# Spreading weight sums over an up-projection, forming one of them in the down stage, and accumulating a row convolution in PSUM by halves

## Chip, cores and metric

The kernel runs on one core of one Trainium2 chip. The metric is the device time of one execution in microseconds (us). Engines are named as in the profile: PE is TensorE, PEld its weight loads, DVE VectorE, ACT ScalarE, POOL GpSimd, SP the engine from whose queue every DMA of this kernel is issued. Each engine works through its instructions in program order.

## What is computed

Two layers of a streaming encoder for 1024 prompt rows and 128 sample rows (8 requests of 16), model width 1024, f32. Each layer has an attention part and the channel mixer on which this change works:

```
def conv_ffn(h, prev, w_up, conv_w, conv_b, w_down):
    u = h @ w_up
    ...
    ue = jnp.concatenate([prev.astype(u.dtype), u], axis=1)
    y = conv_b
    for tap in range(CONV_W):
        y = y + conv_w[tap] * ue[:, tap:tap + T]
    a, g = jnp.split(y, 2, axis=-1)
    out = (jax.nn.gelu(g) * a) @ w_down
    return out, ue[:, T:]
```

The up-projection gives 2 x 2816 columns; a causal convolution of width 3 runs along the rows; one half is gated by the GELU of the other; a down-projection goes back to 1024.

## The kernel before

Every f32 product is made of three matmuls: each operand is split into a high part (a cast, line 177, mostly on ACT) and the rest (a subtraction, line 188, mostly on DVE). Up- and down-projection use a scheme of seven block products in place of eight, which needs sums and differences of weight blocks and of activation blocks.

**The up stage** (`ffn`, layer 0 from about 490 to 1064 us, layer 1 from about 2020 to 2565 us). The 2816 columns are 22 blocks of 128, each a row `a` and a row `g`. The first two blocks are done the plain way (`plain`); the other twenty, j = 2 to 21, are pairs (`spair`). A pair loads two weight tiles through a ring of four tiles, forms the four weight sums S on POOL (lines 1177 to 1180), splits seven operands into a ring of six slots, and PE runs seven products of 24 matmuls (line 1229) into three groups of two PSUM banks, banks 0 to 5. A product's banks are read out (evicted) by ACT (lines 1188 and 1197) or by DVE (line 1190), and within a group the next product accumulates onto the banks only after that. Between the plain blocks and the first pair, `tsums` forms the matching sums of the activations on POOL and DVE.

`conv_row` then does the convolution for one row of 1152: one ACT activation with the third tap and the bias (line 1316), two DVE taps over the 1024 prompt columns (line 1277, called from `conv_row`), and the short taps of the samples with a small POOL addition (line 1286). The `g` row goes through GELU on ACT (line 1323) and a POOL multiplication (line 1324), and the result is stored to DRAM (`actD`). `act_sums` makes the four sums of two finished blocks on POOL (lines 1336 to 1339). In layer 0 `self.ada` runs in the background, four steps to a pair, with loads through the same ring of four tiles and PSUM bank 7.

`weight_sums(m)` makes the sums of the down weights, eleven times in a layer: two loads into the one pair of tiles `w0`, four POOL subtractions of 128 x 512 (lines 1348 to 1351), two stores of 512 KB to DRAM (`wT`). It is called in pairs 2, 3, 4, 6, 8, ..., 20, but it depends on nothing in a pair, and the order of the instructions is set by the tile framework's scheduler from its own timeline, not by the place of the call.

**The down stage** (`down`, 1065 to about 1340 us and 2566 us to the end). Seven products 1, 2, 5, 6, 3, 7, 4 run one after the other, each over eleven m; `fetch(q, m)` loads and splits activation and weight. For product 5 the weight is the difference held in the lower half of `wT[m, 0]`, loaded straight into the slot's low part. In layer 1 the last products run beside the final layer norm of eight row tiles (`head`, `tail`, `norm_last`); `homes` says in which buffer the residual row tile is loaded, and tiles 6 and 7 use the buffers that tiles 2 and 3 used before.

Of the kernel before, what the change touches and what calls it, by code (L numbers as in the profile page):

```python
# [12 lines left out]
AF = mybir.ActivationFunctionType  # L13
ALU = mybir.AluOpType
# [88 lines left out]
class Trunk:  # L103
# [1140 lines left out]
    def ffn(self, l, xsrc, xdst, affs):  # L1244
        nc, I, O, H, F = self.nc, self.I, self.O, self.H, self.F
        nc.sync.dma_start(self.cw, I["cw"][l])
        cw = self.cw.rearrange("p (c w) -> p c w", w=4)
# [22 lines left out]
        wide = Ring(self.ws.items + [F[:, 11644:12668], F[:, 8700:9724]])  # L1270
        narrow = self.ws
        ub = Ring([0, 1, 2, 3, 6, 7])
        UB = ((0, 384), (380, 388), (764, 388))

        def tapper(cc):
            def tap(o, u, i):
                nc.vector.scalar_tensor_tensor(o, u, cw[:, cc, i : i + 1], o, op0=ALU.mult, op1=ALU.add)  # L1277

            return tap

        def samples(y, u, cc, tap):
            y3 = y.rearrange("p (s q) -> p s q", q=16)
            u3 = u.rearrange("p (s q) -> p s q", q=16)
            tap(y3[:, :, 1:16], u3[:, :, 0:15], 1)
            tap(y3[:, :, 2:16], u3[:, :, 0:14], 0)
            nc.gpsimd.tensor_add(y3[:, :, 0:2], y3[:, :, 0:2], E4[:, cc])

        def rows(j, gg, src):
            uo = self.uo[gg].rearrange("p (j s r) -> p j s r", s=9, r=2)
            nc.scalar.copy(uo[:, j % 11], src.rearrange("p (s q) -> p s q", q=16)[:, :, 0:2])  # L1290
            if j % 11 == 10:
                nc.sync.dma_start(O["conv"][l, gg, j // 11], self.uo[gg])
# [20 lines left out]
        def conv_row(u, j, gg, y):  # L1313
            cc = j + 22 * gg
            tap = tapper(cc)
            nc.scalar.activation(y, u[:, 2:1154], AF.Identity, bias=cw[:, cc, 3:4], scale=cw[:, cc, 2:3])  # L1316
            tap(y[:, 0:1024], u[:, 1:1025], 1)
            tap(y[:, 0:1024], u[:, 0:1024], 0)
            samples(y[:, 1024:1152], u[:, 1026:1154], cc, tap)
            rows(j, gg, u[:, 1024:1168])  # L1320

# [22 lines left out]
        def weight_sums(m):  # L1344
            b11, b12, b21, b22 = (t[:, o : o + 512] for t in self.w0 for o in (0, 512))
            for i in range(2):
                nc.sync.dma_start(self.w0[i], I["wdn"][l, 2 * m + i])
            nc.gpsimd.tensor_sub(b11, b12, b11)
            nc.gpsimd.tensor_sub(b12, b22, b12)
            nc.gpsimd.tensor_sub(b22, b22, b11)  # L1350
            nc.gpsimd.tensor_sub(b21, b22, b21)
            for i in range(2):
                nc.sync.dma_start(self.wT[l][m, i], self.w0[i])

        def plain(j):
            y = [yact, ygate[j % 2]]
            for gg in range(2):
                w = self.wload(I["wup"][l, j + 22 * gg])
                for bi, (s0, n) in enumerate(UB):
                    ps = self.bank(ub.next())  # L1360
# [6 lines left out]
        def spair(j):  # L1367
            sa, sg = self.ws.next(), self.ws.next()
            nc.sync.dma_start(sa, I["wup"][l, j])
            nc.sync.dma_start(sg, I["wup"][l, j + 22])  # L1370
            ua, ug = us.next(), us.next()
            y = []

            def after(i, q):
                if i % 2 == 0:
                    self.step(1)
                if i == 1:
                    act_sums()
                if i == 2 and j in wsum:
                    weight_sums(wsum.index(j))  # L1380
                if q == 4:
                    y.append(ygate[j % 2])
                    conv_row(ug, j, 1, y[0])

            self.products(sa, sg, ua, ug, (S1, S2, S3), p1s, sub, TT, after, "first" if j == NPL else None)
            ya = yact
            conv_row(ua, j, 0, ya)
            gated(j, ya, y[0])

        self.pend = []  # L1390
        wsum = [2, 3] + list(range(4, NFF - 1, 2))
# [20 lines left out]
    def down(self, l, xsrc, xdst, affs, act_sums):  # L1412
        nc, I, F, H = self.nc, self.I, self.F, self.H
# [13 lines left out]
        narrow = self.ws  # L1427
        fa, fb = F[:, 4096:5120], F[:, 8320:9344]
        homes = {8: fa, 0: fb, 1: self.w0[1], 2: fa, 3: fb, 4: X2[:, 0:1024], 5: X2[:, 2048:3072], 6: fa, 7: fb}
        xs = {}  # L1430

        def rows(*ts):
# [3 lines left out]
        raws = [w[:, i * 512 : i * 512 + 512] for w in [self.w0[1]] + narrow.items for i in range(2)]  # L1436
        early = Ring(raws + [F[:, o : o + 512] for o in (0, 512, 1024)])
        late = Ring(raws)
        subs = self.subslots(ws[1:4])
        X1 = self.X1  # L1440
        acts = Ring([(X1[:, o : o + 640], X1[:, o + 640 : o + 1280]) for o in range(0, 8960, 1280)])
# [2 lines left out]
        wdn, wT, actD, actS = I["wdn"][l], self.wT[l], self.actD, self.actS  # L1444
        lo_half, hi_half = slice(0, 512), slice(512, 1024)

        def weight(src, ring=None):
            hi, lo = subs.next()
            raw = ring.next() if ring else lo.bitcast(F32)
            nc.sync.dma_start(raw, src)  # L1450
            self.split(raw, hi, lo, "a", "v")
            return hi, lo

        def act(src, sample=None):
            n = 512 if sample is None else 640
            hi, lo = (t[:, 0:n] for t in acts.next())
            raw = lo.bitcast(F32)
            nc.sync.dma_start(raw[:, 0:512], src)
            if sample is not None:
                nc.sync.dma_start(raw[:, 512:640], sample)  # L1460
            self.split(raw, hi, lo, "a", "v")
            return hi, lo
# [12 lines left out]
        def prompt(j, n):  # L1475
            return actD[j][:, n]

        def sample(j):
            return actD[j][:, 1024:1152]

        def fetch(q, m):
            e, o = 2 * m, 2 * m + 1
            w2 = None
            if q == 1:
                a, w = act(prompt(e, lo_half), sample(e)), weight(wdn[e][:, lo_half], early)
            elif q == 2:
                a, w = act(prompt(o, lo_half), sample(o)), weight(wdn[o][:, lo_half], early)
            elif q == 5:
                a, w = act(actS[m, 1][:, hi_half], sample(e)), weight(wT[m, 0][:, lo_half])
                w2 = weight(wdn[e][:, hi_half], late)  # L1490
            elif q == 6:
                a, w = act(actS[m, 0][:, lo_half], sample(o)), weight(wT[m, 1][:, hi_half])
                w2 = weight(wdn[o][:, hi_half], late)
            elif q == 3:
                a, w = act(actS[m, 1][:, lo_half]), weight(wdn[o][:, hi_half], late)
            elif q == 7:
                a, w = act(actS[m, 0][:, hi_half]), weight(wT[m, 0][:, hi_half])
            else:
                a, w = act(prompt(o, hi_half)), weight(wT[m, 1][:, lo_half])
            return a, w, w2 or w  # L1500
# [71 lines left out]
        aff = affs()  # L1572
# [23 lines left out]
        subs = Ring(subs.items + more)  # L1596
# [15 lines left out]
        subs = Ring(subs.items[0 : NK - len(more)] + more if l == 0 else subs.items)  # L1612
# [307 lines left out]
```

## Time and profile before

| | us |
|---|---|
| median of 3 runs | 2839.86 (2837.35 to 2843.75) |
| the profiled execution's own time | 2844.65 |
| its span (first to last instruction) | 2842.6 |
| PE busy in the span | 2676.1 (94%) |
| DVE busy | 2027.0 (71%) |
| ACT busy | 1348.0 (47%) |
| POOL busy | 1106.9 (39%) |
| mean granted PE clock | 0.975 |

All durations below come from the one profiled execution. The parts of its page and the answers of its trace that are used are: busy time by engine in a stretch, groups of instructions by line and shape (count, busy time, mean duration of one, idle time of the engine ahead of them and what ended it), the waits of one engine, and rows in order of time, where a bracket gives the idle time ahead of a row and what released it. F, X2 and H are large SBUF tensors cut up by hand, ws a weight tile, wh and wl the high and low part of a weight, xa an activation part, PS the PSUM banks, C small constants.

### The profile page before, as it was taken

The page shows a single profiled execution, that of the slowest core. Times are in us where ns is not written, and L with a number is a line of the kernel's source. Part 1 is how long each engine was busy: PE and PEld are TensorE (multiplying, and loading weights), DVE is VectorE, ACT ScalarE, POOL GpSimd, SP SyncE. Part 2 cuts the span into 40 slices and gives each one's busy share as a digit, 9 for nine tenths or more (in the row PEclk, how much of TensorE's full clock was granted, in tenths as well). Part 3 has the DMA queues.
Part 4 walks back from the last instruction along what each step waited for, and adds up shares of the span by engine and source line. Part 5 has one row for each costly group of instructions (what it writes and reads, how often), then busy time and mean ns, then how long its engine had stood idle before and what let it go on. Part 6 is the DMA issues. An engine that isn't in the chain of part 4 may idle for free. (4 is left out here: it accounts for less than half of the span.)

```text
span 2842.6 us, 47206 instructions
## 1 busy us (share of the span) xinstructions
PE 2676.1 (94%) x17134; PEld 2356.5 (83%) x17134; DVE 2027.0 (71%) x3850; ACT 1348.0 (47%) x2752; POOL 1106.9 (39%) x808
## 2 busy tenths in 40 slices
PE   7999889889999999999899999999988999999997
PEld 5897768878999997777798888767988999997775
DVE  4376767777776684588663677668888888885578
ACT  3475724433333344455636666652443344444454
POOL 2132523678554641013421111232489855551001
PEclk9999999999999999999999999999999999999998
DMA  8656434698554447675767457854565422237664
GB/s 291 213 159 197 141 129 156 209 329 283 183 175 156 163 133 236 225 248 196 267 201 257 122 156 198 225 162 146 178 206 196 177 81 96 85 116 239 216 218 156
DMA packets 252714, 534.35 MB, mean 188 GB/s; under 512 B 40032, under 2 KB 100400, under 8 KB 252480
## 3 DMA queue, kind: packets, MB, share of 16 engines
q1 hardware_dynamic: 252480, 531.32, 56.8%
q8 instruction: 135, 2.21, 0.3%
q14 instruction: 99, 0.81, 0.1%
HBM read 391.12 MB, written 149.54 MB: 190 GB/s over the span
## 5 line engine op out<-in xcount | busy, mean ns | idle before, releaser
L1229 PE MATMUL PS<-H,wh 128*128 128x256 f32 (+1 forms) x2624 | 409.7, 299 | 0.0
L1466 PE MATMUL PS<-wh,xa 128*128 128x512 f32 x1144 | 366.9, 399 | 11.9 <-DVE F L1584 5.3
L1229 PEld LDWEIGHTS PS<-H,wh 128*128 128x128 f32 x2624 | 374.4, 193 | 0.0
L1277 DVE SCALAR_TENSOR_TENSOR F<-F 128x1024 f32<-128x1024 f32 x320 | 312.9, 1025 | 28.1 <-ACT F L1316 27.8
L177 ACT CAST wh<-F 128x512 fp32r<-128x512 f32 (+2 forms) x234 | 137.1, 594 | 316.5 <-PE PS L1229 203.7
L1190 DVE TENSOR_TENSOR F<-PS,F 128x320 f32<-128x320 f32 (+1 forms) x446 | 196.6, 451 | 123.5 <-PE PS L1229 121.6
L188 DVE TENSOR_TENSOR wl<-F,wh 128x512 fp32r<-128x512 f32 (+2 forms) x234 | 238.6, 1029 | 56.0 <-ACT wh L177 54.3
L1466 PEld LDWEIGHTS PS<-wh,xa 128*128 128x128 f32 x1144 | 215.4, 189 | 69.5 <-ACT H L177 6.1
L1229 PE MATMUL PS<-H,wl 128*128 128x256 f32 (+1 forms) x1312 | 235.4, 301 | 24.4 <-ACT F L1197 15.3
L1466 PE MATMUL PS<-wl,xa 128*128 128x512 f32 x572 | 227.0, 397 | 0.2
L1229 PEld LDWEIGHTS PS<-H,wl 128*128 128x128 f32 x1312 | 196.6, 193 | 34.3 <-ACT F L1197 16.3
L1229 PE MATMUL PS<-xa,wh 128*128 128x320 f32 (+1 forms) x1328 | 207.5, 299 | 0.0
L188 DVE TENSOR_TENSOR xa<-xa 128x640 fp32r<-128x640 f32 (+1 forms) x154 | 122.5, 801 | 112.8 <-ACT xa L177 112.3
L1229 PEld LDWEIGHTS PS<-xa,wh 128*128 128x128 f32 x1328 | 189.8, 192 | 0.0
L1065 POOL TENSOR_TENSOR F<-F 128x1024 f32<-128x1024 f32 x24 | 62.7, 2611 | 308.2 <-ACT xa L177 148.9
L177 ACT CAST xa<-xa 128x640 fp32r<-128x640 f32 (+1 forms) x154 | 104.0, 682 | 162.8 <-DMA xa<-actD 110.8
L188 DVE TENSOR_TENSOR wl<-ws,wh 128x512 fp32r<-128x512 f32 (+1 forms) x149 | 166.2, 1120 | 10.3 <-ACT wh L177 10.2
L1316 ACT ACTIVATE F<-F 128x1152 f32<-128x1152 f32 x80 | 108.0, 1351 | 114.7 <-DVE F L1190 65.7
L177 ACT CAST wh<-ws 128x512 fp32r<-128x512 f32 (+1 forms) x167 | 113.1, 685 | 102.9 <-PE PS L1229 47.1
L640 POOL TENSOR_TENSOR F<-F,x2r 64x512 f32<-64x512 f32 x62 | 79.4, 1280 | 167.9 <-DVE F L616 145.6
L1324 POOL TENSOR_TENSOR F<-F 128x1152 f32<-128x1152 f32 x44 | 123.7, 2810 | 52.1 <-DVE F L1277 40.8
L1229 PE MATMUL PS<-xa,wl 128*128 128x320 f32 (+1 forms) x664 | 122.9, 307 | 21.2 <-DVE F L1190 20.7
(346 smaller groups left out, 6287.3 us busy)
## 6 DMA issues: line engine op xcount, KB each, us to landing
ws<-in_adaw_dram SPq DMA_DIRECT2D x64, 512.0 KB
ws<-in_wup_dram SPq DMA_DIRECT2D x49, 512.0 KB
F<-in_adaw_dram SPq DMA_DIRECT2D x48, 512.0 KB
w0f<-in_wdn_dram SPq DMA_DIRECT2D x44, 512.0 KB
wT<-w0f SPq DMA_DIRECT2D x44, 512.0 KB
actS<-F SPq DMA_DIRECT2D x44, 512.0 KB
xa<-actS SPq DMA_DIRECT2D x88, 256.0 KB
F<-in_wup_dram SPq DMA_DIRECT2D x39, 512.0 KB
```

The source lines that it names most:

```text
L177: nc.scalar.copy(out, in_)
L188: self.eng(el).tensor_sub(lo, src, hi.bitcast(F32))
L640: self.eng("v" if last else "p").tensor_mul(on[r, q], on[r, q], rb[r, :])
L1065: self.eng(er[0]).tensor_mul(xr, x, self.lng)
L1190: nc.vector.tensor_add(d, v(ps), a if len(a.shape) == 3 else v(a))
L1229: self.pairmm = nc.tensor.matmul(ps[:, 0:m], w[a][:, k * 128 : k * 128 + 128], x(p, k, n), start=start and c == 0, stop=c == 11, skip_grou ...
L1277: nc.vector.scalar_tensor_tensor(o, u, cw[:, cc, i : i + 1], o, op0=ALU.mult, op1=ALU.add)
L1316: nc.scalar.activation(y, u[:, 2:1154], AF.Identity, bias=cw[:, cc, 3:4], scale=cw[:, cc, 2:3])
L1324: nc.gpsimd.tensor_mul(yg, yg, ya)
L1466: self.downmm = nc.tensor.matmul(ps, a[p][:, i * 128 : i * 128 + 128], w[q], start=first and c == 0, stop=last and c == 2, skip_group_chec ...
```

## The change

Five edits:

1. `conv_row` no longer does a row in SBUF in one piece. The 128 sample columns get their own activation; the 1024 prompt columns are done in two halves of 512: an ACT activation writes a PSUM bank, one DVE tap accumulates in that bank, and the last tap reads the bank and writes the result to SBUF. The bank is 6 in layer 0, and 6 and 7 in turn in layer 1.
2. `weight_sums` makes three sums instead of four and stores 768 KB instead of 1024.
3. It is tied behind the pair's second weight load with `issue_after`.
4. Product 5 forms the missing difference itself: two loads of plain weight halves into a ring of eight 512-column pieces of F, one POOL subtraction, two splits.
5. In layer 1 the residual tiles 6 and 7 get buffers of their own.

```
+        cb = Ring([6, 7] if l else [6])
...
         def conv_row(u, j, gg, y):
             cc = j + 22 * gg
             tap = tapper(cc)
-            nc.scalar.activation(y, u[:, 2:1154], AF.Identity, bias=cw[:, cc, 3:4], scale=cw[:, cc, 2:3])
-            tap(y[:, 0:1024], u[:, 1:1025], 1)
-            tap(y[:, 0:1024], u[:, 0:1024], 0)
+            aff = dict(bias=cw[:, cc, 3:4], scale=cw[:, cc, 2:3])
+            nc.scalar.activation(y[:, 1024:1152], u[:, 1026:1154], AF.Identity, **aff)
+            for o in (0, 512):
+                ps = self.bank(cb.next())
+                nc.scalar.activation(ps, u[:, 2 + o : 514 + o], AF.Identity, **aff)
+                tap(ps, u[:, 1 + o : 513 + o], 1)
+                nc.vector.scalar_tensor_tensor(
+                    y[:, o : o + 512], u[:, o : o + 512], cw[:, cc, 0:1], ps, op0=ALU.mult, op1=ALU.add
+                )
...
-            nc.gpsimd.tensor_sub(b11, b12, b11)
             nc.gpsimd.tensor_sub(b12, b22, b12)
-            nc.gpsimd.tensor_sub(b22, b22, b11)
+            nc.gpsimd.tensor_add(b22, b12, b11)
             nc.gpsimd.tensor_sub(b21, b22, b21)
-            for i in range(2):
-                nc.sync.dma_start(self.wT[l][m, i], self.w0[i])
+            nc.sync.dma_start(self.wT[l][m, 0][:, 512:1024], b12)
+            nc.sync.dma_start(self.wT[l][m, 1], self.w0[1])
...
-            nc.sync.dma_start(sg, I["wup"][l, j + 22])
+            pairdma = nc.sync.dma_start(sg, I["wup"][l, j + 22]).ins
...
                 if i == 2 and j in wsum:
-                    weight_sums(wsum.index(j))
+                    with self.tc.issue_after(pairdma):
+                        weight_sums(wsum.index(j))
...
+        if l:
+            homes[6], homes[7] = self.hf, self.gateS
...
+        diffs = Ring([F[:, o : o + 512] for o in range(2048, 6144, 512)])
...
             elif q == 5:
-                a, w = act(actS[m, 1][:, hi_half], sample(e)), weight(wT[m, 0][:, lo_half])
-                w2 = weight(wdn[e][:, hi_half], late)
+                a = act(actS[m, 1][:, hi_half], sample(e))
+                r, b = diffs.next(), diffs.next()
+                nc.sync.dma_start(r, wdn[e][:, lo_half])
+                nc.sync.dma_start(b, wdn[e][:, hi_half])
+                nc.gpsimd.tensor_sub(r, b, r)
+                w, w2 = (subs.next() for _ in range(2))
+                self.split(r, *w, "a", "v")
+                self.split(b, *w2, "a", "v")
```

Lines of the changed kernel stand a few higher: 1324 became 1331, 1286 became 1287, the three sums are 1355 to 1357, the activation sums 1343 to 1346, the last tap of a half row 1323, and the split, S sums and evictions keep their numbers.

POOL in the early pairs of layer 1, before. w0f is the pair of tiles of the down weights, the rows on F and ws with 512 columns are the S sums of a pair.

```order
L1348 TENSOR_TENSOR w0f<-w0f 128x512
L1324 TENSOR_TENSOR F<-F 128x1152
L1349 TENSOR_TENSOR w0f<-w0f 128x512
L1350 TENSOR_TENSOR w0f<-w0f 128x512
L1351 TENSOR_TENSOR w0f<-w0f 128x512
L1179 TENSOR_TENSOR F<-F 128x512
L1348 TENSOR_TENSOR w0f<-w0f 128x512
L1177 TENSOR_TENSOR F<-F 128x512
L1286 TENSOR_TENSOR F<-F 128x8x2
L1178 TENSOR_TENSOR F<-F 128x512
L1180 TENSOR_TENSOR F<-F 128x512
L1349 TENSOR_TENSOR w0f<-w0f 128x512
```

The same engine in the repeating part of layer 1 after the change, from one set of down sums on.

```order
L1355 TENSOR_TENSOR w0f<-w0f 128x512
L1356 TENSOR_TENSOR w0f<-w0f 128x512
L1343 TENSOR_TENSOR F<-F 128x512
L1357 TENSOR_TENSOR w0f<-w0f 128x512
L1179 TENSOR_TENSOR F<-ws 128x512
L1344 TENSOR_TENSOR F<-F 128x512
L1177 TENSOR_TENSOR F<-ws 128x512
L1287 TENSOR_TENSOR F<-F 128x8x2
L1345 TENSOR_TENSOR F<-F 128x512
L1178 TENSOR_TENSOR F<-F,ws 128x512
L1287 TENSOR_TENSOR F<-F 128x8x2
L1346 TENSOR_TENSOR F<-F 128x512
```

Before, the eleven sets stand one behind the other from the end of the plain blocks on, between the S sums of the first pairs. After, three sets stand within the first three pairs, and then one comes in every second pair up to pair 20.

DVE around the convolution of a pair in layer 1, before: 1190 are evictions, 188 splits, 1277 the taps.

```order
L1190 TENSOR_TENSOR F<-PS,F 128x5x64
L1277 SCALAR_TENSOR_TENSOR F<-F 128x1024
L1277 SCALAR_TENSOR_TENSOR F<-F 128x8x15
L1190 TENSOR_TENSOR F<-PS,F 128x4x64
L188 TENSOR_TENSOR wl<-F,wh 128x512
L1277 SCALAR_TENSOR_TENSOR F<-F 128x1024
L1277 SCALAR_TENSOR_TENSOR F<-F 128x8x14
L1277 SCALAR_TENSOR_TENSOR F<-F 128x1024
L1277 SCALAR_TENSOR_TENSOR F<-F 128x8x15
L188 TENSOR_TENSOR wl<-F,wh 128x512
L1190 TENSOR_TENSOR F<-PS,F 128x5x64
```

The same place after; line 1278 is now the tap.

```order
L188 TENSOR_TENSOR wl<-F,wh 128x512
L1323 SCALAR_TENSOR_TENSOR F<-F,PS 128x512 x2
L1190 TENSOR_TENSOR F<-PS,F 128x5x64
L1190 TENSOR_TENSOR F<-PS,F 128x4x64
L1278 SCALAR_TENSOR_TENSOR PS<-F,PS 128x512
L188 TENSOR_TENSOR wl<-ws,wh 128x512
L1323 SCALAR_TENSOR_TENSOR F<-F,PS 128x512
L1278 SCALAR_TENSOR_TENSOR PS<-F,PS 128x512
L1323 SCALAR_TENSOR_TENSOR F<-F,PS 128x512
```

The pieces are half as long, twice as many, and each first one of a half stands behind an ACT activation; evictions and splits are put between the halves.

SP at the end of layer 1, before: xd is the residual in DRAM, out_y_dram the output.

```order
L1019 DMA out_y_dram<-w0f 128x1024
L1458 DMA xa<-actD 128x512
L1450 DMA wl<-wT_105 128x512
L1458 DMA xa<-actD 128x512
L1450 DMA H<-wT_105 128x512
L1019 DMA out_y_dram<-F 128x1024
L1458 DMA xa<-actD 128x512
L1450 DMA H<-wT_105 128x512
L1081 DMA F<-xd_99 128x1024
L1458 DMA xa<-actD 128x512 x4
L1019 DMA out_y_dram<-F 128x1024
L1081 DMA F<-xd_99 128x1024
```

The same place after.

```order
L1019 DMA out_y_dram<-w0f 128x1024
L1468 DMA xa<-actD 128x512
L1460 DMA H<-wT_105 128x512
L1468 DMA xa<-actD 128x512
L1460 DMA H<-wT_105 128x512
L1019 DMA out_y_dram<-F 128x1024
L1468 DMA xa<-actD 128x512 x4
L1019 DMA out_y_dram<-F 128x1024 x2
```

The two residual loads of tiles 6 and 7, each behind the output store of the tile whose buffer it takes, are gone from this place; they stand some 40 to 50 rows earlier.

## Prediction

> **What bounds the kernel now.** I read the busy times first, then the stretches, then the waits in the stretches that are slow.
>
> ```profile
> PE 2676.1 (94%) x17134; PEld 2356.5 (83%) x17134; DVE 2027.0 (71%) x3850; ACT 1348.0 (47%) x2752; POOL 1106.9 (39%) x808
> POOL 2132523678554641013421111232489855551001
> ```
>
> PE is the bound, and only time in which it stands can be won. POOL's row of 40 slices has two humps (7, 8 in slices 9 and 10; 8, 9, 8 in slices 30 to 32), both at the start of an up stage. To see what they cost, I cut the up stages at the eviction of the first product of a pair, one in each pair. Rows: start, duration, engine, line.
>
> ```profile
> 547.43 0.42 ACT L1197 COPY F<-PS 128x320 f32<-128x320 f32 x1
> 750.11 0.41 ACT L1197 COPY F<-PS 128x320 f32<-128x320 f32 x1
> 1048.17 0.41 ACT L1197 COPY F<-PS 128x320 f32<-128x320 f32 x1
> 2086.16 0.42 ACT L1197 COPY F<-PS 128x320 f32<-128x320 f32 x1
> 2278.23 0.42 ACT L1197 COPY F<-PS 128x320 f32<-128x320 f32 x1
> 2547.03 0.42 ACT L1197 COPY F<-PS 128x320 f32<-128x320 f32 x1
> ```
>
> These are pairs 2, 9 and 21 of each layer. Layer 0: 12 pairs in 298.06 us, 24.84 each; the seven before them 202.68, which is 28.8 above 7 x 24.84 = 173.9. Layer 1: 268.80 / 12 = 22.40; the seven before them 192.07, which is 35.3 above 156.8. Together **64.1 us**. The same stretches by engine (length; busy time of PE, PEld, DVE, ACT, POOL; PE clock, DMA share, GB/s):
>
> ```profile
> 547.40:750.10 202.70, 187.15 (x1423) 170.91 (x1424) 147.46 (x184) 66.61 (x114) 156.33 (x110) 0.96 0.80 280
> 750.10:1048.20 298.10, 297.79 (x2323) 277.91 (x2321) 219.21 (x310) 115.09 (x195) 159.93 (x114) 1.00 0.45 151
> 2086.20:2278.20 192.00, 171.48 (x1192) 168.94 (x1193) 167.06 (x179) 65.58 (x114) 170.22 (x110) 0.94 0.52 187
> 2278.20:2547.00 268.80, 268.80 (x2018) 268.68 (x2017) 229.23 (x301) 112.06 (x194) 151.91 (x105) 1.00 0.27 94
> ```
>
> In the late stretches PE never stands and the clock is 1.00. In the early ones POOL is at 77 and 89%, DVE at 73 and 87%, PE stands 16 and 21 us, and its clock is 0.96 and 0.94. What PE waits for, layer 0 and then layer 1 (us in all, times, longest):
>
> ```profile
> PE PS L1229 <- ACT F L1197: 8.8, 3, 6.9
> PE PS L1229 <- DVE wl L188: 6.4, 3, 5.7
> PE PS L1229 <- DVE F L1190: 3.9, 4, 1.9
> PE PS L234 <- DMA ws<-in_adaw_dram: 1.9, 1, 1.9
> ```
>
> ```profile
> PE PS L1229 <- DVE F L1190: 20.1, 10, 5.6
> PE PS L1229 <- ACT F L1197: 6.4, 1, 6.4
> ```
>
> Late evictions, on DVE. Why DVE is late there: its groups, early and then late in layer 1 (count, busy, mean ns).
>
> ```profile
> L188 DVE TENSOR_TENSOR wl<-F,wh 128x512 fp32r<-128x512 f32 x37 | 49.4, 1342 | 8.9 <-ACT wh L177 8.0 <-issue 0.9
> L1277 DVE SCALAR_TENSOR_TENSOR F<-F 128x1024 f32<-128x1024 f32 x26 | 45.9, 1764 | 2.6 <-ACT F L1316 2.6
> L1190 DVE TENSOR_TENSOR F<-PS,F 128x320 f32<-128x320 f32 x36 | 17.3, 482 | 3.1 <-PE PS L1229 3.1
> ```
>
> ```profile
> L1277 DVE SCALAR_TENSOR_TENSOR F<-F 128x1024 f32<-128x1024 f32 x49 | 71.2, 1453 | 11.7 <-ACT F L1316 11.7
> L188 DVE TENSOR_TENSOR wl<-F,wh 128x512 fp32r<-128x512 f32 x60 | 58.0, 975 | 6.1 <-ACT wh L177 6.1
> L1190 DVE TENSOR_TENSOR F<-PS,F 128x320 f32<-128x320 f32 x60 | 29.0, 483 | 5.4 <-PE PS L1229 5.4
> ```
>
> Operations with two SBUF sources stretch with POOL's load (1453 to 1764, 975 to 1342); those that read PSUM and one SBUF tensor do not (483, 482). What loads POOL early are the sums of the down weights:
>
> ```profile
> L1349 POOL TENSOR_TENSOR w0f<-w0f 128x512 f32<-128x512 f32 x10 | 19.8, 1984 | 2.9 <-DMA w0f<-in_wdn_dram 2.8
> L1350 POOL TENSOR_TENSOR w0f<-w0f 128x512 f32<-128x512 f32 x10 | 16.8, 1678 | 0.2
> ```
>
> Four such operations in ten of the eleven sets, some 70 us of the 170.
>
> **The change part by part.** *Sums spread.* After, pairs 5 to 8 carry at most one set in two pairs. Of the 64.1 us I leave 6 in each layer for the first pair: its order makes PE wait for an eviction right behind its product, and it starts cold after the standstill of 6.9 or 6.4, as these rows show (8 matmuls of 320 columns each):
>
> ```profile
> 549.14 2.33 PE L1229 MATMUL PS<-H,wh 128*128 128x320 f32 x8
> 554.44 1.33 PE L1229 MATMUL PS<-H,wh 128*128 128x320 f32 x8
> ```
>
> I leave 3 in each layer for the three sets that still come in pairs 2 to 4, and 3 in layer 0 for waits of the background work (1.9 in the row on adaw). Won: 64.1 - 12 - 6 - 3 = **43**. The standstill before the first pair itself I leave as it is: tsums and the first set still meet there (0, bounds -5 to +3).
>
> *One sum fewer.* 22 POOL operations less, 22 stores of 512 KB halved. POOL after, per pair of layer 1: 151.91 / 12 = 12.7, and 11 sets x 3 x 1.7 over 20 pairs = 2.8, so 15.5 of 22.4. It stays clear of the bound; 0 by itself.
>
> *The row by halves.* The trace before has no operation that writes PSUM from DVE or ACT. The nearest rows are the taps of the plain blocks, which read PSUM, and two activations:
>
> ```profile
> L1277 DVE SCALAR_TENSOR_TENSOR F<-PS,F 128x384 f32<-128x384 f32 x6 | 3.7, 612 | 0.1
> L1277 DVE SCALAR_TENSOR_TENSOR F<-PS,F 128x256 f32<-128x256 f32 x5 | 2.4, 472 | 0.0
> L1316 ACT ACTIVATE F<-F 128x1152 f32<-128x1152 f32 x80 | 108.0, 1351 | 114.7 <-DVE F L1190 65.7 <-POOL F L1286 15.9 <-DMA actS<-F 13.4
> L938 ACT ACTIVATE F<-F,C 128x128 f32<-128x128 f32 x64 | 25.4, 483 | 10.9 <-DMA F<-hmD 10.9
> ```
>
> DVE: 140 ns for 128 columns gives 0.75 us at 512. Out go four taps a pair, 4 x 1.45 = 5.8; in come eight at 0.75 = 6.0: +0.2, and 229.23 / 12 = 19.1 becomes 19.3 of 22.4. Bounds for one of the new taps: 0.61 (the 384 row) and 1.45 (a whole old tap); at 1.45 for all eight DVE would need 24.9 and would be the bound in layer 1, 2.5 us a pair. I take 0.75, the nearest rows. ACT: 868 ns for 1024 columns, so 0.81 at 512; a row costs 0.48 + 2 x 0.81 = 2.10 in place of 1.35, 1.5 a pair, 9.3 + 1.5 = 10.8 of 22.4 (bounds 0.67 to 1.35 for a half). The cover is PE's 22.4; without it 1.5 x 40 = 60 us would show. What the edit gives is room: in the late stretch of layer 1 four long DVE operations a pair no longer hold or await POOL, so late evictions get rarer there, where PE already never stands: 0.
>
> [...]
>
> The added waits: DVE's tap stands behind ACT's write of the half, and in layer 0 the next activation behind DVE's last tap on the one bank; evictions and splits are queued behind both, and PE behind the evictions. An eviction has one product to be done in, 22.4 / 7 = 3.2 us. Activation, tap and last tap are 0.81 + 0.75 + 0.75 = 2.3. That fits once, so I take 0.
>
> *Product 5.* Same loads and splits; 11 POOL operations a layer where POOL's slices read 1, 0, 1 and 1, 0, 0, 1: 0. PE's waits in that stage of layer 1 are few:
>
> ```profile
> PE PS L1466 <- DVE F L1584: 3.0, 1, 3.0
> PE PS L1466 <- ACT wh L177: 0.9, 2, 0.7
> ```
>
> They could move by 3 either way. *Buffers for tiles 6 and 7.* At the end ACT waits for the load of tile 7, tile 4's variance behind it, and DVE for that:
>
> ```profile
> 2817.32 1.06 ACT L1530 ACTIVATE F<-F 128x1024 f32<-128x1024 f32 x1 [11.47 <-DMA F<-xd]
> 2819.55 0.15 DVE L1009 TENSOR_SCALAR C<-C 128x1 f32<-128x1 f32 x1 [1.85 <-ACT F L1008]
> 2818.91 3.66 PE L1466 MATMUL PS<-H,xa 128*128 128x512 f32 x15
> 2826.02 2.83 DVE L1534 CUSTOM_DVE_ANT_0 F<-F 128x512 f32<-128x512 f32 x1
> ```
>
> The 1.85 goes. Next late is PE's end at 2822.6, behind which DVE's work on tile 7 and POOL's on 4 and 5 stay, the 2.83 among them: **-1** (bounds -4 to +2).
>
> **Sum.** -43 - 1 = -44: the profiled execution's 2844.65 would be 2800.6. It lies 4.8 above the median of the runs; from the median 2839.86 I predict **2796**.
>
> **Rivals.** (a) *Other queues keep part of it.* The new stores wait for POOL in SP's queue ahead of weight loads, and in layer 0 loads are already late:
>
> ```profile
> L1177 POOL TENSOR_TENSOR F<-F 128x512 f32<-128x512 f32 x6 | 8.3, 1381 | 24.3 <-DMA F<-in_wup_dram 24.3
> ```
>
> 4 us late in each of six without PE standing, so there is some slack. If every second pair from 5 on loses 2 us in layer 0, 16 go: 2812. (b) *The sums were not it*: the standstills follow tsums and cold restarts, and spreading gives half: 2818. For: layer 0's 5.7 comes from one split. Against: the excess runs through seven pairs and ends with the last set. (c) *All of it comes*, and half of the 6.9 + 6.4 in front: 2839.9 - 64 = 2776. (d) *Slower: DVE waits for the bank.* If each half finds two evictions ahead on ACT, DVE stands 0.81 + 2 x 0.42 = 1.65 for each of four halves: 19.3 + 6.6 = 25.9 a pair in layer 1. Its 19 periods then take 492 for the 461 of now: +31, and layer 0 wins 10 instead of 17: about 2860. Layer 1 starts to lose at 0.8 a half, the whole at about 1.5. For: DVE already waits for ACT's whole row (11.7 in the late stretch). Against: that is 0.5 a row, and the rows between the halves are DVE's own work.
>
> **Chances.** Forecast 0.47, (a) 0.18, (b) 0.12, (c) 0.13, (d) 0.10. About 0.2% is what a measurement of this kernel can tell from no change. All but (d) are faster, with 0.03 of (b) within: faster 0.87, same 0.03, slower 0.10. The range takes in (b) with 9 us on it, (c), and the bounds of the small terms: 2773 to 2827; it leaves out (d) and the bound of 1.45.
>
> **What the profile after would show.** Right: the first seven periods at 23 to 26 us, no hump in POOL's slices, PE clock 0.98 or more there; DVE halves near 0.75 both alone and beside POOL; DVE under 21 a pair late in layer 1; no wait of ACT for tile 7. Wrong: halves above 1 us, evictions late in the pairs 9 to 21 where PE never stood, DVE waiting for line 1321, SP's weight loads waiting behind wT.

## The result, and the profile after

| | before | after |
|---|---|---|
| median of the runs side by side | 2838.61 us (2834.37 to 2843.75) | 2815.36 us (2812.51 to 2817.75) |
| ratio, with its 95% interval | | 0.9909 [0.9888, 0.9930] |
| the same kernels run a second time | 2839.85 | 2819.31, ratio 0.9931 [0.9914, 0.9948] |
| span of the profiled execution | 2842.6 | 2811.8 |

The change wins 21 to 23 us. 44 were forecast.

Every kernel of this study issues the same 17134 matmuls in very nearly the same order. So the start of PE's n-th matmul is a better mark than an eviction, which can move against PE. I cut at the numbers 3360 (the plain blocks of layer 0), 4704, 7056 (the last pair), 8400 (behind the down stage), 12700, 13776, 15900 and 17133 (the last). The changed kernel between these marks (length; busy time of PE, PEld, DVE, ACT, POOL; PE clock, DMA share, GB/s):

```profile
527.90:719.90 192.00, 177.53 (x1347) 163.71 (x1346) 139.61 (x219) 75.57 (x144) 101.45 (x83) 0.96 0.65 223
719.90:1020.80 300.90, 300.90 (x2354) 279.65 (x2353) 234.06 (x360) 128.82 (x242) 178.77 (x135) 1.00 0.56 191
1020.80:1336.40 315.60, 295.74 (x1347) 240.23 (x1346) 229.70 (x368) 157.97 (x276) 63.49 (x35) 0.98 0.66 217
1336.40:2056.50 720.10, 684.79 (x4301) 591.08 (x4300) 484.47 (x1202) 410.82 (x919) 205.50 (x162) 0.98 0.62 193
2056.50:2219.00 162.50, 149.37 (x1079) 148.15 (x1078) 140.92 (x212) 72.66 (x140) 98.54 (x80) 0.96 0.40 139
2219.00:2506.40 287.40, 284.48 (x2126) 283.33 (x2125) 250.29 (x364) 131.50 (x252) 172.98 (x131) 1.00 0.38 132
2506.40:2790.90 284.50, 275.52 (x1235) 224.19 (x1234) 194.39 (x327) 142.34 (x238) 35.54 (x25) 0.98 0.65 211
```

The two early parts (first and fifth row) by the same marks in the kernel before:

```profile
535.10:735.40 200.30, 178.32 (x1346) 163.51 (x1345) 151.05 (x199) 68.76 (x120) 152.18 (x109) 0.95 0.82 286
2070.00:2257.20 187.20, 158.81 (x1079) 155.77 (x1078) 166.53 (x186) 66.28 (x117) 164.76 (x109) 0.92 0.56 197
```

POOL's load there is down from 76 and 88% to 53 and 61%, DVE's only from 75 and 89% to 73 and 87%: DVE has 11 and 26 us less to do, in a stretch that is 8 and 25 us shorter. The page of the changed kernel has no hump left:

```profile
POOL 2132523456555642112420122242465656542101
```

What PE waits for in the early part of layer 0, then of layer 1, then in the late part of layer 1 (us in all, times, longest):

```profile
PE PS L1229 <- ACT F L1197: 6.9, 1, 6.9
PE PS L1229 <- DVE wl L188: 5.7, 3, 4.2
PE PS L1229 <- DVE F L1190: 1.9, 1, 1.9
```

```profile
PE PS L1229 <- ACT F L1197: 8.9, 1, 8.9
PE PS L1229 <- DVE F L1190: 4.1, 4, 2.6
```

```profile
PE PS L1229 <- DVE F L1190: 2.7, 3, 1.7
```

In layer 1 the 20.1 us of late DVE evictions have become 4.1. The standstill ahead of the first pair stays in both layers (6.9 as before in layer 0, 8.9 where it was 6.4 in layer 1). In layer 0 a wait of 4.2 for one split stays too. And late in layer 1, where PE never stood, it now stands three times. There the new operations cost what was expected; DVE and then ACT:

```profile
L188 DVE TENSOR_TENSOR wl<-F,wh 128x512 fp32r<-128x512 f32 x65 | 76.8, 1190 | 3.2 <-ACT wh L177 3.2
L1278 DVE SCALAR_TENSOR_TENSOR PS<-F,PS 128x512 f32<-128x512 f32 x49 | 36.5, 744 | 0.0
L1323 DVE SCALAR_TENSOR_TENSOR F<-F,PS 128x512 f32<-128x512 f32 x49 | 35.7, 739 | 7.1 <-DMA actS<-F 6.8
L188 DVE TENSOR_TENSOR wl<-ws,wh 128x512 fp32r<-128x512 f32 x25 | 32.7, 1307 | 0.0
```

```profile
L1321 ACT ACTIVATE PS<-F 128x512 f32<-128x512 f32 x49 | 38.1, 777 | 57.6 <-DVE F L1323 35.4 <-DVE F L1190 22.1
```

The taps on the bank take 0.74 us. Of the 160 that accumulate in it, the 108 that no POOL operation overlaps have a median of 746 ns, the 31 that lie wholly within one 747. (Before, a tap of 1024 had a median of 1277 ns with POOL idle, and of 1918 where POOL worked all through it.) DVE waits for ACT's half nowhere there; ACT waits for DVE, but no wait of PE there ends with ACT. What still stretches is the splits, 1190 and 1307 ns (the median of the 32 with no POOL operation beside them is 682). They did before too, in the same part and with no down sums beside them:

```profile
L188 DVE TENSOR_TENSOR wl<-F,wh 128x512 fp32r<-128x512 f32 x65 | 64.4, 1000 | 6.9 <-ACT wh L177 6.9
L188 DVE TENSOR_TENSOR wl<-ws,wh 128x512 fp32r<-128x512 f32 x25 | 38.3, 1533 | 0.0
```

Together they take 109.5 us where they took 102.7.

### The profile page after: what moved, and what is told of

It is laid out like the page before. It is cut to its first block, busy times and chain, and to the rows that moved or that the text cites. A ratio compares the mean times of both kernels' runs of the same rounds, so it can differ in the third digit from the quotient of the medians.

```text
span 2811.8 us, 47453 instructions
## 1 busy us (share of the span) xinstructions
PE 2657.6 (95%) x17134; PEld 2341.9 (83%) x17134; DVE 2031.0 (72%) x4010; ACT 1393.4 (50%) x2912; POOL 1031.4 (37%) x808
## 4 chain that ended last, share of the span: by engine, by line
PE 69%; DVE 11%; DMA 10%; POOL 4%; issue 3%; ACT 3%; SPq 1%; DVEq 0%; POOLq 0%; ACTq 0%
PE PS L1229 26%; PE PS L1476 15%; PE PS L319 10%; PE PS L306 7%; PE PS L602 2%; PE PS L580 2%; DVE wl L188 2%; PE PS L234 2%; PE PS L551 1%; DMA w0f<-in_wdn_dram 1%; PE PS L293 1%; DMA actS<-F 1%; DMA ws<-in_adaw_dram 1%; DVE F L518 1%; PE PS L554 1%
## 5 line engine op out<-in xcount | busy, mean ns | idle before, releaser
L188 DVE TENSOR_TENSOR wl<-F,wh 128x512 fp32r<-128x512 f32 (+2 forms) x278 | 274.2, 996 | 31.6 <-ACT wh L177 29.1
L177 ACT CAST wh<-F 128x512 fp32r<-128x512 f32 (+2 forms) x278 | 163.7, 598 | 219.4 <-PE PS L1229 132.5
L1321 ACT ACTIVATE PS<-F 128x512 f32<-128x512 f32 x160 | 124.6, 779 | 187.6 <-DVE F L1323 107.2
L177 ACT CAST wh<-ws 128x512 fp32r<-128x512 f32 (+1 forms) x153 | 104.3, 691 | 97.8 <-PE PS L1229 30.2
L188 DVE TENSOR_TENSOR wl<-ws,wh 128x512 fp32r<-128x512 f32 (+1 forms) x135 | 135.7, 1011 | 8.4 <-ACT wh L177 7.9
L319 PE MATMUL PS<-xa,H 128*128 128x512 f32 x504 | 133.3, 405 | 6.2 <-ACT xa L177 3.3
L306 PE MATMUL PS<-H,w0r 128*128 128x384 f32 (+1 forms) x720 | 138.3, 342 | 0.0
```

Source lines behind the costliest of these rows:

```text
L177: nc.scalar.copy(out, in_)
L188: self.eng(el).tensor_sub(lo, src, hi.bitcast(F32))
L306: mm = self.nc.tensor.matmul(out[:, 0:n], w[a][:, k * 128 : k * 128 + 128], H[:, p, k, s0 : s0 + n], start=i == 0, stop=i == 23)
L319: self.nc.tensor.matmul(out[:, 0:n], H[:, p, j * kn + k, t0 : t0 + 128], w[a][:, k * n : k * n + n], start=i == 0, stop=i == 23,)
L1321: nc.scalar.activation(ps, u[:, 2 + o : 514 + o], AF.Identity, **aff)
```

## The experiments

All stages below are lengths between the marks, as differences from the mean of two profiles of the kernel before, in us. The part ahead of mark 3360 is left out, since it moves by itself (second group). The last columns are the sum of the stages, and the medians side by side.

| kernel | up 0 early | up 0 late | down 0 | between | up 1 early | up 1 late | down 1 | tail | sum | medians | ratio |
|---|---|---|---|---|---|---|---|---|---|---|---|
| before, two profiles | 200.5 | 301.4 | 305.9 | 726.9 | 186.9 | 283.5 | 281.2 | 20.0 | | | |
| the whole change, two profiles | -8.2 | -0.5 | +10.0 | -5.0 | -25.6 | +4.4 | +4.2 | +0.8 | -20 | -23, -21 | 0.9909, 0.9931 |
| spread alone | -8.6 | +5.8 | +6.1 | -1.7 | -18.9 | +18.5 | +2.2 | +0.7 | +4 | -3 | 0.9995 [0.9982, 1.0007] |
| halves alone | -1.9 | -0.2 | +8.0 | +0.5 | -20.0 | -0.4 | +0.7 | +0.4 | -13 | -13 | 0.9954 [0.9937, 0.9972] |
| three sums and product 5 alone | +2.0 | 0.0 | +7.4 | -3.2 | -6.6 | +1.3 | -2.2 | +0.2 | -1 | -1 | 0.9999 [0.9980, 1.0018] |
| all but the spread | +0.6 | -0.1 | +12.1 | -2.4 | -20.2 | -0.4 | +0.2 | +0.8 | -9 | -9 | 0.9967 [0.9954, 0.9980] |
| whole, halves in SBUF | -6.5 | +13.8 | +1.8 | -5.7 | -15.6 | +38.5 | +2.7 | +0.4 | +29 | +27 | 1.0099 [1.0082, 1.0116] |
| whole, one tap in SBUF | -8.3 | +0.3 | +6.9 | -6.5 | -22.3 | +33.5 | +8.8 | +0.4 | +13 | +8 | 1.0035 [1.0017, 1.0052] |
| whole, y written first | -13.6 | +1.9 | +16.6 | -5.8 | -29.7 | -0.4 | -0.6 | +0.4 | -31 | -34 | 0.9877 [0.9861, 0.9893] |
| whole, sets later | -20.4 | +0.3 | +15.5 | -6.4 | -32.5 | +4.1 | +6.1 | +0.7 | -33 | -38 | 0.9869 [0.9851, 0.9888] |
| both of these | -15.6 | +7.6 | +13.5 | -2.9 | -32.6 | +2.6 | +2.8 | +0.4 | -24 | -26 | 0.9915 [0.9897, 0.9932] |
| both, pair 20 of layer 0 as before | -18.8 | +11.0 | +10.7 | -6.4 | -34.9 | +1.6 | +6.0 | +0.4 | -30 | -35 | 0.9879 [0.9860, 0.9899] |

### Which part of the change won

My theory: the sets crowd POOL in the first pairs, DVE's operations with two SBUF sources stretch beside them (the tap of 1024 from 1277 to 1918 ns), and spreading is the gain (the crowding theory). The rival: the gain is the bank's, whose taps don't stretch (746 ns away from POOL, 747 beside it).

**Spread alone.**

```
+                    with self.tc.issue_after(pairdma):
+                        weight_sums(wsum.index(j))
```

> The kernel before with the sums tied behind the second weight load of their pair, and nothing else: four sums, taps of 1024 in SBUF, product 5 as before. Crowding theory (the sums beside DVE's two-source operations are what makes the early pairs slow): the first seven periods of layer 1 fall from 192 to 165-172 and those of layer 0 from 203 to 188-194, so 2838 becomes 2805-2815, at least as good as the whole change. Halves theory (the change won because its taps no longer wait for POOL): 2830 or more, early periods of layer 1 above 180. On the loss behind the up stage of layer 0 (PE gave back 9 us there in the whole change): if the sums that now come late cause it, PE waits at the start of the down stage of layer 0 here too, 5 us or more over before; if product 5's new loads and subtraction cause it, nothing is lost there.

Measured: 2837.18, no difference. Both halves of the sum are visible. The early parts win 27.5, near the whole change's 33.8, and the late parts give 24.3 back. In the late pairs of layer 1 POOL does a set in every second pair. By the eviction of the first product these pairs take 26.0 and those without 21.9; before, without a set in either, the same pairs took 23.8 and 21.0 in turn, so two pairs lose 3.1. A piece of one of them shows how (start, duration, engine, line, and in the bracket the idle time ahead and its releaser):

```profile
2357.52 1.35 ACT L1316 ACTIVATE F<-F 128x1152 f32<-128x1152 f32 x1 [4.09 <-POOL F L1339]
2358.77 0.68 ACT L1197 COPY F<-PS 128x320 f32<-128x320 f32 x2
2358.79 1.28 POOL L1180 TENSOR_TENSOR ws<-ws,F 128x512 f32<-128x512 f32 x1
2358.90 2.25 DVE L1277 SCALAR_TENSOR_TENSOR F<-F 128x1024 f32<-128x1024 f32 x1 [2.56 <-ACT F L1316]
2359.23 0.59 PEld L1229 LDWEIGHTS PS<-H,wl 128*128 128x128 f32 x4 [1.66 <-ACT F L1197]
2359.23 0.85 PE L1229 MATMUL PS<-H,wl 128*128 128x320 f32 x4 [1.45 <-ACT F L1197]
```

ACT wants to write the row into the y buffer, but POOL's last activation sum (line 1339) still works on that buffer, late because the four operations of a set stand between the activation sums in POOL's queue. Two evictions stand behind ACT, and PE behind them. What PE waits for in the late part of layer 1:

```profile
PE PS L1229 <- ACT F L1197: 8.7, 5, 2.9
PE PS L1229 <- DVE F L1190: 5.5, 9, 1.5
```

So the crowding theory holds for the early pairs and fails for the sum: there was no room in the late ones.

**Halves alone.**

```
+            for o in (0, 512):
+                ps = self.bank(cb.next())
...
```

> The kernel before with the row convolution by halves in PSUM, and nothing else: all eleven sets still in the first seven pairs. Crowding theory: the splits and the S sums still meet the sets, so the early periods fall by a third at most (192 to 180-190 in layer 1): 2828-2840. Halves theory: the early periods of layer 1 fall to 165-172, 2805-2818. If the halves cost something in the late pairs, their twelve periods in layer 1 go from 268.8 to 271 or more here too; if the late 2.8 us of waits in the whole change come from the spread sums, they stay at 268.8.

Measured: 2827.30, -13. With all eleven sets still in the first seven pairs, layer 1's early part falls by 20.0, as much as by spreading. Layer 0's hardly moves. Both theories had a part of it right: either cure does most of the same 25 us in layer 1. The late parts are untouched (-0.2, -0.4), so the 4.4 that the whole change loses late in layer 1 is not the halves' alone; it comes with the spread sums. What PE waits for in the early part of layer 1 here; the 20.1 of before for line 1190 is gone, with the sets on POOL as they were:

```profile
PE PS L1229 <- ACT F L1197: 12.3, 4, 8.2
PE PS L1229 <- DVE F L1190: 2.7, 2, 2.3
PE PS L1229 <- DVE F L1278: 0.3, 1, 0.3
```

**Three sums and product 5 alone.**

```
-            nc.gpsimd.tensor_sub(b22, b22, b11)
...
+                nc.gpsimd.tensor_sub(r, b, r)
```

> The kernel before with three sums in place of four and product 5 forming its difference, and nothing else: sets still crowded. Crowding theory: a quarter of POOL's extra work is gone in the first seven pairs, so a quarter of the 64 us of surplus, about 10-16 us less there; if product 5's loads and subtraction cause the loss of 9 us in the down stage of layer 0 and 3 in that of layer 1, it shows here: 2833-2840 in all. If they don't: 2823-2829.

Measured: 2838.62, no difference. 6.6 come in layer 1, none in layer 0, less than the 10 to 16 that the crowding theory asked for, and 7.4 are lost in the down stage of layer 0.

**All but the spread.**

> The whole change without the tie behind the second weight load: three sums, halves in PSUM, product 5 and the buffers, with the sets crowded into the first seven pairs. Crowding theory: most of the gain is gone, 2828-2838, early periods of layer 1 above 178. Halves theory: nearly all of the gain stays, 2812-2820, early periods of layer 1 at 172 or less.

Measured: 2831.24, -9. The whole lies where the crowding theory put it, the early part of layer 1 (166.7) where the halves theory did. With the bank in place the spread is worth some 12 us more, alone it was worth nothing: the spread needs the bank. The bank gains without the spread.

### How steady the stages are

**Before and after once more**, unchanged, for second profiles.

> The kernel before once more, for a second profile. If the 9 us that the changed kernel lost behind the up stage of layer 0 (from PE's 7056th to its 8400th matmul: 306.2 before, 315.6 after, and 312.0 to 318.0 in all four of the partial kernels) are the change's, this profile shows 305-308 there; if the first profile of before was a quick one at that place, it shows 311-316. The 7 us that the changed kernel gained ahead of the first up stage (529.4 and 522.2) should likewise be absent from the code: 526-531 here.

> The changed kernel once more, beside the others on one chip: 2812-2819, with the stages of its first profile within 1 us (191.9, 301.0, 162.5, 287.4 in the up stages) and only the part ahead of the first up stage free to move, as it was between the two profiles of before.

Each stage of before repeated within 1.0 us, but the part ahead of mark 3360 was 11 us shorter. After repeated within 1.0 in layer 0's up stage and the down stage behind it, within 2.3 in layer 1's up stage and the last down stage, and within 3.7 between the layers. The loss of 10 behind the up stage of layer 0 is real.

The profiled executions of before and after first shown differ by 31 us for this reason: 7 of it lies ahead of the first up stage.

### What the bank gives the late pairs

The spread needs the bank. Two theories: a tap with an operand in the bank doesn't stretch beside POOL (the 746 and 747 ns), or the y buffer is needed later.

**Halves in SBUF**: the whole change, but the halves lie in y.

```
-                ps = self.bank(cb.next())
+                ps = y[:, o : o + 512]
```

> The changed kernel, but the two halves of a row accumulate in their place in SBUF and not in a PSUM bank; all else as changed. If it is the PSUM operand that makes room in the late pairs (taps out of POOL's reach, and ACT free to begin while the y buffer is still being read), the late part of the up stage of layer 1 goes back to 297-303 us as in the kernel with the spread alone (302.0, against 287.4 in the changed kernel), and the whole to 2830-2838. If it is the half length alone (shorter pieces that let evictions through), 285-290 there and 2814-2820.

Measured: 2867.14, +27, beyond both expectations. The length of the pieces is not it. The late part of layer 1 takes 322.0; DVE there is busy 289.15 of it:

```profile
L1323 DVE SCALAR_TENSOR_TENSOR F<-F 128x512 f32<-128x512 f32 x50 | 54.6, 1091 | 0.0
L1278 DVE SCALAR_TENSOR_TENSOR F<-F 128x512 f32<-128x512 f32 x49 | 51.0, 1040 | 0.1
L188 DVE TENSOR_TENSOR wl<-ws,wh 128x512 fp32r<-128x512 f32 x25 | 47.0, 1879 | 2.8 <-ACT wh L177 2.8
```

and ACT waits there for the y buffer:

```profile
ACT F L1321 <- POOL F L1346: 38.1, 5, 7.9
```

Both causes are present, so this kernel doesn't part them.

**One tap in SBUF**: ACT writes the bank, the first tap reads it and writes y, the last works in y.

```
-                tap(ps, u[:, 1 + o : 513 + o], 1)
+                nc.vector.scalar_tensor_tensor(
+                    y[:, o : o + 512], u[:, 1 + o : 513 + o], cw[:, cc, 1:2], ps, op0=ALU.mult, op1=ALU.add
+                )
...
+                tap(y[:, o : o + 512], u[:, o : o + 512], 0)
```

> The changed kernel, but of the two taps of a half only the first reads the bank (it writes y), and the last has both operands in SBUF; ACT still writes the bank and is as free of the y buffer as in the changed kernel. If POOL's hold on operations with two SBUF sources is what the bank avoids, those last taps take 1.0-1.1 us on average in place of 0.74 (as both taps do in the kernel with SBUF halves: 1.04 and 1.09), and about half of that kernel's loss comes: the late part of layer 1 goes from 287 to 297-308, the whole to 2828-2845. If ACT's waiting for the y buffer (38 us for line 1346 in that kernel) was the loss, the late part stays at 285-291 and the whole at 2812-2822.

Measured: 2847.60, +8; the late part of layer 1 takes 317.0, beyond both expectations. The taps in SBUF take 868 ns, less than I expected, and DVE's busy time there is only 7.1 above that of the changed kernel (257.40 against 250.29). The rest is a wait that I had not thought of. This edit moves the first write of y from the last tap to the first, and DVE now stands for POOL's sum as ACT did:

```profile
DVE F L1322 <- POOL F L1346: 24.0, 6, 4.1
```

with the evictions behind it; PE waits 19.4 us for line 1190 in seven times. So in DVE's time the buffer is the larger part and the stretch the smaller, 24 and 7. The part is 29.6 us longer than in the changed kernel, more than PE's waits, since the matmuls behind a standstill were slower (one of the seven; eight of 320 columns take 2.13 us behind it and 1.34 ahead of it):

```profile
2341.17 1.34 PE L1229 MATMUL PS<-H,wh 128*128 128x320 f32 x8
...
2346.90 1.44 PE L1229 MATMUL PS<-xa,wl 128*128 128x320 f32 x4 [2.96 <-DVE F L1190]
2348.14 2.13 PE L1229 MATMUL PS<-xa,wh 128*128 128x320 f32 x8
```

PE is busy for 297.41 us there, at a granted clock of 0.96, where it was 284.48 at 1.00. A standstill so cost more than its own length: 16.7 us more of waits came with 12.9 us of slower matmuls.

**Y written first**: PSUM as changed, but ACT writes one column of y's upper half ahead of the halves, and they are kept behind it.

```
+            first = nc.scalar.activation(y[:, 1023:1152], u[:, 1025:1154], AF.Identity, **aff).ins
...
+                with self.tc.issue_after(first):
+                    nc.scalar.activation(ps, u[:, 2 + o : 514 + o], AF.Identity, **aff)
```

> The changed kernel with one more column in the sample activation (column 1023, written again by the last tap), and the halves' activations kept behind it on ACT: PSUM and all durations as changed, but ACT may begin a row only when POOL's activation sums and their stores have let go of the upper half of the y buffer, as the row of 1152 had to before. If the waiting for that buffer was what the halves took away (ACT waited 4.1 us in one pair for line 1339 with the spread alone), the late part of layer 1 takes 295-303 us and the whole 2824-2834. If POOL's hold on two-source operations was it, 286-290 and 2814-2819.

Measured: 2805.65, a gain and not a loss. The added wait is there (12.3 us for the stores of y, in five times), but PE never stands in the late part of layer 1 (283.0 of 283.0 busy). The tie gave the scheduler another order. An eviction stands behind each of the five waits here too, 2.3 us on, but its product ends only then: it starts 0.03 to 0.9 us after the product's end. With one tap in SBUF the evictions behind the waits start 2.4 to 2.6 us after it. DVE's splits also met POOL less:

```profile
L188 DVE TENSOR_TENSOR wl<-F,wh 128x512 fp32r<-128x512 f32 x65 | 63.0, 970 | 8.3 <-ACT wh L177 8.3
L1324 DVE SCALAR_TENSOR_TENSOR F<-F,PS 128x512 f32<-128x512 f32 x50 | 36.9, 738 | 0.2
...
L188 DVE TENSOR_TENSOR wl<-ws,wh 128x512 fp32r<-128x512 f32 x25 | 19.1, 763 | 0.0
```

970 and 763 ns in place of 1190 and 1307, with the same load on POOL; they run beside it for 49 us in place of 73. So waiting for y need not cost. In these runs it cost where the wait held up an eviction whose product was done. The waits were shorter here too (3.1 at most, against 4.1), so the order is not the only thing that differs. How the loss with halves in SBUF is shared between the stretch and the wait stays open: a second y buffer would tell it, and was not tried.

### Can more be had

**Sets later**: nothing of the sums in the transition and the first two pairs.

```
-        wsum = [2, 3] + list(range(4, NFF - 1, 2))
+        wsum = list(range(NFF - 18, NFF - 4, 2)) + list(range(NFF - 4, NFF))
```

> The changed kernel with the first sets taken out of the transition: they are called in pairs 4, 6, 8, ..., 16, 18, 19, 20, 21. If the sets in the first three pairs still cost what the first periods have above 25 and 23 us (2 + 9 in layer 0, 6 + 4 in layer 1) and part of the standstills of 6.9 and 8.9 ahead of them, the early parts fall from 191.9 to 180-187 and from 162.5 to 153-158, less 1 to 2 us a pair for the four sets in a row at the end: 2800-2810. If those periods come from tsums, the cold clock and POOL's other work (its S sums of the second pair stood behind two conv rows, not behind a set), nothing is won: 2813-2818.

Measured: 2802.20, ratio 0.9869 to before. The three sets in the transition and the first pairs cost 12 us in layer 0 and 7 in layer 1 (180.1 and 154.4 in place of 192.3 and 161.4). Of this, 1.8 and 3.7 lie in the standstills ahead of the first pair, now 5.1 and 5.2. The split that PE waited 4.2 us for is no longer late; what PE waits for in the early part of layer 0:

```profile
PE PS L1229 <- ACT F L1197: 5.1, 1, 5.1
PE PS L1229 <- DVE wl L188: 0.7, 1, 0.7
PE PS L261 <- DVE F L253: 0.3, 1, 0.3
```

**Both edits.**

> The changed kernel with both of the edits that won by themselves: sets called in pairs 4 to 16, 18, 19, 20, 21, and the halves' activations behind the sample activation. If the two gains (13 us and 10 us) are separate places (the first three pairs; order in the late pairs), 2790-2798, with 154 and 283 us in layer 1. If they are the same place, 2799-2806.

Measured: 2813.49, no better than the whole change and outside both ranges. Layer 1's early part keeps the gain and layer 0's most of it (15.6 of 20.4). At the end of layer 0's up stage PE stands twice, 6.2 us ahead of mark 7056 and 9.3 behind it. The gains don't add.

**Both, and pair 20 of layer 0 in one piece.**

> The kernel with both edits, and the rows of pair 20 in layer 0 alone done in one piece in SBUF as before. If the time lost at the end of layer 0's up stage (PE waits 7.0 and 8.0 us for one eviction behind splits of the down stage, in the two kernels with one of the edits, and 1.9 + 1.8 + 1.6 in the changed one) comes from the half rows of pair 20 pushing the evictions of pair 21 back in DVE's queue, PE waits 2 us or less there and the whole is 5 to 8 us under the kernel with both edits. If DVE is late there for another reason (one split of the down stage beside POOL's long multiplication), it is within 2 us.

Measured: 2805.03, 8.5 less than with both edits. But by the stages only 3 of that lie at the place (up 0 late, down 0 and between); 8 of the 14 us between the two profiles lie ahead of mark 3360. PE's waits behind mark 7056 are 5.2 where they were 9.3, but the one ahead of it is 7.8 where it was 6.2. So the half rows of pair 20 are a small part of that loss at most.

## Why the prediction was half right

The prediction named the right place and a direction, its range held the time, and the gain was half of its 44. By the stages the 24 that are missing are 9 in the early pairs, 10 behind the up stage of layer 0, 4 late in layer 1, 4 in the last down stage and 2 at the end, less 5 that came unforecast between the layers. Its parts in turn:

- **The early pairs, 43.** 33.8 came. Layer 1: 25.6 of 26.3. Layer 0: 8.2 of 16.8. I left only 3 in each layer for the three sets that stay in pairs 2 to 4, and 6 for the first pair. With these sets moved on, 12 and 7 more come. A set in the transition meets tsums on POOL and the first splits on DVE, and one in a later pair meets neither. So the term for three remaining sets was mis-sized, 6 where moving them gave 19; 5.5 of the 19 lie in the standstills ahead of the first pairs, which the prediction had left as they were. Rival (b) put the excess down to tsums and cold restarts (before, PE's granted clock is 0.50 from 549.1 to 551.5 us, behind the standstill, and 1.00 from 554.4 to 555.8); against that, 20.4 of layer 0's excess of 28.8 went with the sets.
- **"At the late pairs 0."** The row by halves was to give "room ... where PE already never stands: 0". This is the step of the reasoning that failed. Early I had counted what the sets take there; I did not count what they take where they go. Alone, the spread costs 24.3 late and is worth nothing. The bank was worth 13 us by itself and makes the spread worth some 12 more. In the whole change 4.4 of that price remains in layer 1, with late evictions in its late pairs (2.7 us in three times), which the prediction had named as a sign of being wrong.
- **The halves.** Sizes right: 0.74 for 0.75, the activation 0.78 for 0.81, DVE 20.0 us a pair late in layer 1 for "under 21". With no POOL operation beside them, a row's taps take 2.97 us where they took 2.55 (two of 746 and two of 739 ns for two of 1277), 0.42 more. DVE was not the bound (late in layer 1 it is busy for 250.29 of 287.40 us), and halves alone lose nothing there (-0.4). A tap on the bank is as long beside POOL as away from it, the 747 and 746 ns above; with both operands in SBUF 1277 became 1918. Rival (d), DVE waiting for the bank, did not come: in the late pairs of layer 1 DVE waits for line 1321 nowhere, and ACT waits for DVE.
- **The seam behind the up stage of layer 0, costed at nothing: +10.0.** In the changed kernel PE waits there; the row of before at the same place was 0.2:

```profile
PE PS L1229 <- DVE F L1190: 3.6, 2, 1.9
PE PS L1476 <- ACT wh L177: 1.6, 1, 1.6
PE PS L1476 <- DVE wl L188: 0.4, 1, 0.4
```

  DVE's queue now has splits of the down stage ahead of the last evictions, and one of them takes 2.76 us beside POOL's long multiplication (2.69 us); the median with POOL idle is 0.83:

```profile
1039.93 2.76 DVE L188 TENSOR_TENSOR xa<-xa 128x640 fp32r<-128x640 f32 x1 [0.85 <-ACT xa L177]
1042.61 0.68 DVE L188 TENSOR_TENSOR wl<-ws,wh 128x512 fp32r<-128x512 f32 x1
1043.21 0.48 DVE L1190 TENSOR_TENSOR F<-PS,F 128x320 f32<-128x320 f32 x1
```

  These waits are 5.4 of the 10. One more, of 2.7 us for an ACT eviction (line 1590), follows some 50 us later; before had one of 1.8 near there. About 3 come back just behind mark 8400, where waits stand a little earlier than before. The first waits go with the bank: by PE's matmul 7296 the two profiles of the changed kernel have lost 6.2 and 5.8 since mark 7056, halves alone 4.8 and all but the spread 7.9, but the spread alone, the three sums alone and the halves in SBUF 1.2 at most. The spread alone (6.1 by mark 8400) and the three sums alone (7.4) lose theirs later. I can't divide the rest of the 10, nor the 4.2 in the last down stage, where three sums and product 5 alone won 2.2.
- **The end, -1.** The wait of ACT for tile 7's load is gone, as forecast, but no time went with it: 20.8 us from PE's last matmul to the end, where it was 20.0. The 2.83 us on DVE beside POOL's multiplication (line 1017) is there as before; the median of this operation is 0.72. Tiles 6 and 7 were not what the end waited for.
- **The rivals.** (b) gave 2818 and (a) 2812, both within 4 of the measured 2815, and neither by its mechanism: their nearness is luck. For (b), see the early pairs above. For (a), nothing was lost in pairs 5 to 8, whose periods are 25.4 in layer 0 (four of 26.5, 24.4, 25.5, 25.3), or in the late part (-0.5). The sum of (c) leaves out the half of the standstills that it names; with it (c) is 2769, not 2776. The PE clock that I wanted as a sign (0.98 or more early) came to 0.96 in both layers, from 0.95 and 0.92 by the same marks: the first pair still starts after a standstill, and PE still waits in the pairs behind it.

## What to carry to other kernels

Work moved off a crowded place has to be priced where it lands, on the same engine and with the same instructions beside it; "PE never stands there" is a statement on the load of before. An intermediate in PSUM gave two things here: a DVE tap that does not stretch beside POOL (747 ns beside it, 746 away from it), and a later first write to a buffer that another engine still uses. And where a scheduler fixes the order, look at what stands behind each new wait on its engine, and whether it is due: 24 us of waits on DVE with due evictions behind them went with 19 us of waits on PE, 12 us on ACT with an eviction behind them that was not yet due cost PE nothing. With one tap in SBUF PE's standstills also cost more than they lasted: 12.9 us of slower matmuls came with 16.7 us more of waiting.

## What the runs showed of the hardware

Two executions of the same kernel before differed by 11 us ahead of the first up stage and by 2 in all the rest. The time lies in three short stretches in which PE did the same work at a lower granted clock (0.83, 0.87 and 0.88, where the second profile has 1.00). In the largest of them, the stretch from PE's 600th to its 700th matmul, the first profile and then the second have:

```profile
104.90:125.00 20.10, 16.70 (x106) 14.29 (x99) 10.28 (x38) 10.67 (x35) 0.29 (x2) 0.83 0.55 176
```

```profile
105.20:119.90 14.70, 14.13 (x107) 11.65 (x100) 9.30 (x35) 10.28 (x33) 0.29 (x2) 1.00 0.65 214
```

0.83 against 1.00, and 5.4 us: 2.6 of it is slower matmuls, 2.8 is longer standing, for DVE results. What made the two differ, no run shows. Two profiles of one kernel tell which stages of a single comparison can be trusted.
